# A two-layer decoder trunk: late modulation sums of layer 0 behind dt's chain, layer 1's first chunk by pieces of h, scale columns at once

## The chip, the cores and the metric

One core of a Trainium2 chip runs the kernel. The metric is device time in microseconds (us) of one launch, the median of several runs. The engines are TensorE (PE in the profile; PEld are its weight loads), VectorE (DVE), ScalarE (ACT), GpSimd (POOL), and SyncE (SP), on whose queue the loads are issued.

## The reference, cut to what matters

The input is 256 tokens of width 1024, all in float32. Two layers follow each other, and both do this:

```python
cond = silu(c)
mod = cond @ ada_w[l] + ada_b[l]              # 6 x 1024: sh1, sc1, g1, sh2, sc2, g2
h = rms_norm(x, norm1_g[l]) * (1 + sc1) + sh1
z, xbc, dt_raw, mq, mk, mv, sq, sk, sv = split(h @ w_in[l])
y_ssd  = ssd_mixer(z, conv(xbc), softplus(dt_raw + bias), ...)   # two chunks of 128 tokens
y_moba = moba_attention(mq, mk, mv)           # with 256 tokens: plain causal attention, 4 heads
y_swa  = swa_attention(sq, sk, sv)            # window 128, with sinks, 4 heads
x = x + g1 * (concat(rms_norms of the three) @ w_out[l])
h = rms_norm(x, norm2_g[l]) * (1 + sc2) + sh2
x = x + g2 * peer_ffn(h)                      # 8 heads, top 16 of 128 x 128 experts
```

A last RMSNorm follows.

## The kernel before

**Tiling.** Channels lie on partitions in eight blocks of 128 (KD = 8), tokens in two blocks (NC = 2). Products in float32 are made in two ways. The first projections of a layer multiply float32 as it is (`proj_parts_whole`, `proj_tokens_whole`, lines 360 and 375). All others split each operand into a high and a low part in fp32r: `split` (lines 165 to 177) copies the high part on ScalarE and subtracts for the low part, on VectorE in layer 1 and on GpSimd in layer 0 (`low_of`), and `mm3` multiplies three times (lines 180 to 182). `hs` holds the two parts of h, `wH` and `wL` those of a weight chunk, with three buffers each; `raw` holds loaded chunks in five.

**Modulations.** They are dot products on VectorE. `ada_ahead` (lines 194 to 213) makes a list of steps; one step issues the load of a weight tile of 512.5 KB three steps ahead and then one VectorE instruction (line 192), called a sum here, which multiplies the tile by the conditioning row and accumulates one column of `modc`. Layer 0 has 40 such steps in its mixers: 16 early ones (shift and scale of the first norm) and 24 late ones (m = 2, the gate of the mixers; m = 3 and 4, shift and scale of the second norm), eight columns each. Their tiles use four buffers (tags oH and oL, two each), which the last two splits of w_out use later. Layer 1's sums run in layer 0's expert stage, so layer 1's mixers have none.

**The first chunk.** h is made in four pieces p of two blocks: `norm_banks` transposes on PE into one bank, `norm_h` first makes a scale column (line 264) and then h from the bank, half on VectorE (line 284) and half on ScalarE (line 282). In layer 0 the early steps are spread over the four pieces, and five weight chunks (`WHOLE0`) are multiplied by each piece as it comes. In layer 1 the table `FIRST` says which step of the chunks mq, mk and sq goes ahead of a piece and which behind it; mq is multiplied as it is, mk and sq by high and low parts, whose `halves` of h are made in between (lines 290 and 291).

**The late steps.** After the first chunk `tick` is set to `later` (line 586), and each weight chunk that is then loaded calls it (lines 326, 354, 371), which runs two late steps (RATE). In layer 0 that starts in the stage `rest`, which computes dt and the values of attention (`values_dt`, line 609). `rest` has four chunks, so eight late steps are traced ahead of dt's chain (lines 612 to 631). The output projection calls `later` four times more (line 745).

**Order.** `ORDER` names the stages in the order in which they are traced: c0 to c3 the convolutions, mv and mp the values and output of the first attention, ss, sv and sp the scores, values and output of the second, seg the decays, z0 and z1 the gate, tok, stb, cb and st the SSD steps. What is traced first has precedence; a planner, which simulates the time of each instruction, puts one queue in order for each engine, and an engine runs its queue in that order. `tc.issue_after(i)` puts the instructions of its block behind i in the queue of the engine of i. Loads are all on SP's queue, where one that waits for its buffer holds up those behind it. Loads of `rest` are issued behind the last load of a sum that was asked for by then (line 369).

**Around it.** The output projection (lines 731 to 760) needs the gate row from m = 2; the second norm (lines 761 to 766) needs m = 3 and 4. Layer 1 starts with the end of layer 0's expert stage: lines 1080 to 1085 add it to x, and `norm_rows` and `norm_scaled` make the rows of the norm.

Of the kernel before, what the change touches and what calls it, by code (L numbers as in the profile page):

```python
# [13 lines left out]
F32 = mybir.dt.float32  # L14
# [3 lines left out]
ALU = mybir.AluOpType  # L18
# [4 lines left out]
P = 128  # L23
D = 1024
S = 256
NC = 2
KD = D // P
# [12 lines left out]
NCAND = 80  # L40
GH = 4
RB = 5
RATE = 2.0
PT = (0, 0)
CV = (1, 0)
WHOLE0 = "mq mk sq xbc0 xbc1"
FIRST = (
    ((WHOLE0, WHOLE0), ("", WHOLE0), (WHOLE0, WHOLE0), ("", WHOLE0)),
    (("- - - mq", "mq"), ("mk mk - sq sq", "mq mk sq"), ("mq - mk -", "mq mk"), ("sq sq", "mq mk sq")),
)  # L50
ORDER = (
    "rest c0 c1 mv ss mp seg c2 z0 sv c3 tok stb z1 cb st sp",
    "rest c0 mv c1 mp seg ss c2 z0 sv c3 tok stb z1 cb st sp",
)
low_of = ["h"]
# [21 lines left out]
COLS = {"adab": 0, "n1": 48, "n2": 56, "cw": 64, "cb": 96, "mg": 104}  # L77
# [13 lines left out]
def trunk(ctx: ExitStack, tc: tile.TileContext, x_in, c_in, ada, cols, rows, w_in, w_out, wq, keysT, uT, vT, fg, out, dbg=None):  # L91
    nc = tc.nc
    V, A, G, T = nc.vector, nc.scalar, nc.gpsimd, nc.tensor
# [3 lines left out]
    st = ctx.enter_context(tc.tile_pool(name="st", bufs=2))  # L97
# [56 lines left out]
    def fetch_whole(src):  # L154
# [7 lines left out]
        nc.sync.dma_start(t[:, :n], src)  # L162
        return t[:, :n]

    def split(src, low="v", pool=None):
        n = src.shape[-1]
        if pool is None:
            h = st.tile([P, 1024], F32R, tag="wH", name="wH", bufs=HB)
            lo = st.tile([P, 1024], F32R, tag="wL", name="wL", bufs=HB)
        else:  # L170
            h = pool.tile([P, D + 1], F32R, tag="oH", name="oH", bufs=2)
            lo = pool.tile([P, D + 1], F32R, tag="oL", name="oL", bufs=2)
        A.copy(h[:, :n], src)  # L173
        eng, step = (V if low == "v" else G), (n // 2 if low == "h" else n)
        for o in range(0, n, step):
            eng.tensor_tensor(out=lo[:, o:o + step], in0=src[:, o:o + step], in1=h[:, o:o + step].bitcast(F32), op=ALU.subtract)  # L176
        return h, lo

    def mm3(o, l, r, start, stop):
# [59 lines left out]
    whole2, whole2_halves = [], []  # L239
# [3 lines left out]
    def pinned():  # L243

        return tc.issue_after(pin[0]) if PIN else nullcontext()

    def norm_scaled(pool, xt, c, r):
        t = pool.tile([P, D], F32, tag="sc", name="xn", bufs=2)
        for n in range(2):
            V.tensor_scalar(out=t[:, n * 512:(n + 1) * 512], in0=xt[:, c, n * 512:(n + 1) * 512], scalar1=r, scalar2=None, op0=ALU.mult)  # L250
        return t

    def norm_banks(xn, k20=0, n=KD // 2, kind=None):
        banks = [bank(kind) for _ in range(n)]
        for c in range(NC):
            for k in range(2 * k20, 2 * (k20 + n)):
                o = k % 2 * S + c * P
                T.transpose(banks[k // 2 - k20][:, o:o + P], xn[c][:, k * P:(k + 1) * P], ident)
        return banks

    def norm_h(pool, banks, colt, modc, gcol, sh, sc, k20=0, whole=None, keep32=None):
        k0, n = 2 * k20, 2 * len(banks)
        acol = pool.tile([P, KD], F32, tag="acol", name="acol")
        V.scalar_tensor_tensor(out=acol[:, k0:k0 + n], in0=modc[:, sc, k0:k0 + n], scalar=1.0, in1=colt[:, gcol + k0:gcol + k0 + n], op0=ALU.add, op1=ALU.mult)
        halves = []
        for k2 in range(k20, k20 + len(banks)):
            if keep32 is not None:
                h32 = keep32.tile([P, 2, S], F32, tag="wt", name="h32", bufs=KD // 2)
            elif whole is None or k20 or len(banks) == 1:
                h32 = pool.tile([P, 2, S], F32, tag="t2k", name="h32", bufs=3)  # L270
            elif k2 % 2 == 0:
                four = st.tile([P, 1024], F32, tag="wL", name="h32", bufs=HB).rearrange("p (k t) -> p k t", k=4)
                h32 = four[:, 0:2, :]
            else:
                h32 = four[:, 2:4, :]
            if whole is not None:
                whole.append(h32)
            for q in range(2):
                k = 2 * k2 + q
                src = banks[k2 - k20][:, q * S:(q + 1) * S]  # L280
                if q and H32A:
                    A.activation(h32[:, q, :], src, AF.Identity, scale=acol[:, k:k + 1], bias=modc[:, sh, k:k + 1])
                else:
                    d = V.tensor_scalar(out=h32[:, q, :], in0=src, scalar1=acol[:, k:k + 1], scalar2=modc[:, sh, k:k + 1], op0=ALU.mult, op1=ALU.add)
                    done[0] = d.ins
                    if whole is not None and len(banks) > 1:
                        pin[0] = d.ins

            def half(k2=k2, h32=h32):
                A.copy(hs[0][:, 2 * k2:2 * k2 + 2, :], h32)  # L290
                V.tensor_tensor(out=hs[1][:, 2 * k2:2 * k2 + 2, :], in0=h32, in1=hs[0][:, 2 * k2:2 * k2 + 2, :].bitcast(F32), op=ALU.subtract)
            if whole is None:
                half()
            else:
                halves.append(half)
        return halves
# [19 lines left out]
    tick = [lambda: None]  # L316
# [74 lines left out]
    def mixers(l, xp, mx, xt, xn, modc, colt, early, late):  # L391
        if True:
# [54 lines left out]
            o = 0  # L447
# [69 lines left out]
                    put_y(self.yn, self.blk0, 2)  # L517

            todo = list(late)
            due = [0.0]  # L520

            def later():
                due[0] += RATE
                while todo and due[0] >= 1.0:
                    due[0] -= 1.0
                    todo.pop(0)()

            xbcT = new([P, 8, S], "xbcT")

# [22 lines left out]
            if l:  # L552
                first = {n: [bank(b) for b in kinds] for n, kinds in (("mq", ("pa", "pa")), ("mk", ("pa", "pa")), ("sq", ("pb", "pb")))}
                part = {n: proj_parts(pcs, wl, *off[n], 2) for n, pcs in first.items()}
                whole = []
                part["mq"] = proj_parts_whole(first["mq"], wl, *off["mq"], 2, whole)
            else:
# [4 lines left out]
                for n in WHOLE0.split():  # L562
# [2 lines left out]
                    first[n] = [pc[:, b * S:(b + 1) * S] for b in range(2)]  # L565
                    part[n] = proj_parts_whole(first[n], wl, *off[n], 2, whole, True)
            halves = []
            for p, names in enumerate(FIRST[l]):
                banks = norm_banks(xn, p, 1, "pc")
                pre, post = names  # L570
                pre = pre.split()
                ada = early[4 * p:4 * p + 4]
                for i in range(max(len(pre), len(ada))):
                    if i < len(ada):
                        ada[i]()
                    if i < len(pre) and pre[i] != "-":
                        with pinned() if p == 1 else tc.issue_after(asked[0]) if p == 2 and l == 0 else nullcontext():
                            next(part[pre[i]])
                halves += norm_h(xp, banks, colt, modc, COLS["n1"], 0, 1, p, whole, None if l else mx)
                for n in post.split():  # L580
                    next(part[n])
                    while l and halves:
                        halves.pop(0)()
            for g in part.values():
                assert next(g, None) is None
            tick[0] = later
            if l == 0:
                proj_tokens_rest = lambda: proj_tokens_whole(wl, *off["rest"], whole)
            else:
# [19 lines left out]
            def values_dt():  # L609

                for c, pc in enumerate(proj_tokens_rest()):
                    V.tensor_tensor(out=dtp[:, c, :], in0=pc[:, 0:8], in1=rowt[:, 0:8], op=ALU.add)
                    A.copy(vx[:, c, :, 0:64], pc[:, 8:392].rearrange("p (h d) -> p h d", d=64))


                na = new([P, NC, 8], "na")
                V.tensor_scalar(out=na, in0=dtp, scalar1=-1.0, scalar2=None, op0=ALU.mult)
                V.tensor_tensor(out=na, in0=na, in1=dtp, op=ALU.min)
                ey = new([P, NC, 8], "ey")
                A.activation(ey, na, AF.Exp)  # L620
                e1 = new([P, NC, 8], "e1")
                V.tensor_scalar(out=e1, in0=ey, scalar1=1.0, scalar2=None, op0=ALU.add)
                er = new([P, NC, 8], "er")
                V.tensor_scalar(out=er, in0=e1, scalar1=1.0, scalar2=None, op0=ALU.subtract)
                V.tensor_tensor(out=er, in0=ey, in1=er, op=ALU.subtract)
                A.activation(e1, e1, AF.Ln)
                V.tensor_tensor(out=er, in0=er, in1=e1, op=ALU.add)
                V.scalar_tensor_tensor(out=dt, in0=dtp, scalar=0.0, in1=er, op0=ALU.max, op1=ALU.add)
                ah = new([P, 8], "ah")
                A.activation(ah, rowt[:, 8:16], AF.Exp)  # L630
                V.scalar_tensor_tensor(out=a, in0=dt, scalar=-1.0, in1=ah[:, None, :].to_broadcast([P, NC, 8]), op0=ALU.mult, op1=ALU.mult)

            def decays():

# [55 lines left out]
            def swa_scores():  # L690
# [12 lines left out]
                "sv": lambda: att["s"].values(), "sp": lambda: att["s"].put(),  # L703
                "c0": lambda: conv(0), "c1": lambda: conv(1), "c2": lambda: conv(2), "c3": lambda: conv(3),
                "z0": lambda: gate_z(0), "z1": lambda: gate_z(1),
                "seg": decays, "tok": tokens, "stb": state_in, "cb": scores_cb, "st": state,
            }
            for name in ORDER[l].split():
                stages[name]()
# [53 lines left out]
                    gated_add(xp, xt, c, n, pcs[n][c], gb)  # L763
                xn.append(norm_scaled(xp, xt, c, norm_rows(xp, xt, c)))
            whole2[:] = []
            whole2_halves[:] = norm_h(xp, norm_banks(xn), colt, modc, COLS["n2"], 3, 4, 0, whole2)


    def peer(l, steps):
# [391 lines left out]
```

## Time and profile before

| | |
|---|---|
| median of 3 runs | 1942.69 us (1938.9 to 1942.85) |
| profiled execution | 1945.66 us, span 1943.9 us |
| PE busy | 1879.8 us, 97% of the span |
| DVE, ACT, POOL busy | 72%, 48%, 22% |
| mean granted clock of TensorE | 0.983 of full speed |

A busy share is a mean over the whole span. The forty slices of the profile's page (48.6 us each) show where PE is less busy: among the first four slices, and in two from 972 us on, where layer 1 starts. A row of the view of stretches gives from and to, the length, the busy time of PE, PEld, DVE, ACT and POOL with the number of records, the granted clock as a share of full speed, the share of the transfer engines and what they moved. In a timeline a row gives the start in us, the length in us, engine and line, what is written from what, and how many instructions in a row were merged; in square brackets stand the idle time ahead of it and what ended it. A float32 matmul has two records. Sums leave two entries in the trace, the product and the reading of the accumulator.

### The profile page before, as it was taken

The numbers are of one execution on the slowest core, as the hardware profiler recorded it, in microseconds if no ns is written. First come the engines' busy times: TensorE is split into PE (matmuls) and PEld (weight loads), VectorE is DVE, ScalarE is ACT, GpSimd is POOL, SyncE is SP. The second block draws the span as 40 slices with busy tenths as digits, with TensorE's granted clock in tenths as the row PEclk, the third lists the DMA queues.
The fourth block names the chain that finished last, engine by engine and source line by source line (L and its number), as shares of the span: only waits on it lengthen the run. The fifth ranks groups of instructions, "written<-read, shape, count | busy, mean of one in ns | idle before, by whom it ended". The sixth has DMA issues, their size and how long they took to land. (4 is left out here: it accounts for less than half of the span.)

```text
span 1943.9 us, 33211 instructions
## 1 busy us (share of the span) xinstructions
PE 1879.8 (97%) x12714; PEld 1707.9 (88%) x12714; DVE 1403.6 (72%) x2686; ACT 939.6 (48%) x1473; POOL 420.2 (22%) x255
## 2 busy tenths in 40 slices
PE   7798999999999999999989899999999999999998
PEld 5577999999999888888878789999999998888886
DVE  5955897889963898966657659968899346666665
ACT  2453545544444544545537444455444444555554
POOL 1263789100014001000001147960000320000000
PEclk8889999999999999999999999999999999999999
DMA  9833455444455999865543344554444555665563
GB/s 351 323 126 123 163 167 189 165 158 155 161 165 183 373 357 346 319 205 195 194 129 113 128 148 161 186 184 153 162 154 162 175 184 194 224 196 194 192 194 118
DMA packets 103984, 377.55 MB, mean 194 GB/s; under 512 B 12049, under 2 KB 12305, under 8 KB 103313
## 3 DMA queue, kind: packets, MB, share of 16 engines
q1 hardware_dynamic: 103824, 375.43, 57.1%
q8 instruction: 99, 1.62, 0.4%
q14 instruction: 61, 0.49, 0.1%
HBM read 372.24 MB, written 3.15 MB: 193 GB/s over the span
## 5 line engine op out<-in xcount | busy, mean ns | idle before, releaser
L173 ACT CAST wH<-raw 128x1024 fp32r<-128x1024 f32 x577 | 602.6, 1045 | 517.2 <-PE pu L181 349.1
L176 DVE TENSOR_TENSOR wL<-raw,wH 128x1024 fp32r<-128x1024 f32 (+1 forms) x435 | 532.9, 1226 | 215.7 <-ACT wH L173 214.7
L180 PE MATMUL pu<-hH,wH 128*128 128x256 f32 x2048 | 581.1, 284 | 6.0 <-ACT act L791 6.0
L182 PE MATMUL pu<-hH,wL 128*128 128x256 f32 x2048 | 575.7, 281 | 0.0
L181 PE MATMUL pu<-hL,wH 128*128 128x256 f32 x2048 | 575.3, 281 | 0.0
L176 POOL TENSOR_TENSOR wL<-raw,wH 128x1024 fp32r<-128x1024 f32 (+1 forms) x178 | 365.2, 2071 | 641.0 <-ACT wH L173 620.9
L181 PE MATMUL pacc<-wL,aH 128*128 128x512 f32 x1008 | 393.3, 390 | 0.0
L180 PEld LDWEIGHTS pu<-hH,wH 128*128 128x128 f32 x2048 | 386.4, 189 | 6.8 <-ACT act L791 6.8
L182 PE MATMUL pacc<-wH,aL 128*128 128x512 f32 x1008 | 392.4, 389 | 0.0
L181 PEld LDWEIGHTS pu<-hL,wH 128*128 128x128 f32 x2048 | 386.9, 189 | 0.0
L182 PEld LDWEIGHTS pu<-hH,wL 128*128 128x128 f32 x2048 | 386.6, 189 | 0.0
L180 PE MATMUL pacc<-wH,aH 128*128 128x512 f32 x1008 | 272.5, 389 | 0.0
L999 ACT CAST aH<-act 128x256 fp32r<-128x256 f32 x256 | 103.5, 407 | 323.5 <-PE pacc L181 323.5
L180 PEld LDWEIGHTS pacc<-wH,aH 128*128 128x128 f32 x1008 | 189.3, 188 | 39.5
L182 PEld LDWEIGHTS pacc<-wH,aL 128*128 128x128 f32 x1008 | 189.3, 188 | 39.1
L181 PEld LDWEIGHTS pacc<-wL,aH 128*128 128x128 f32 x1008 | 189.3, 188 | 38.9
L1000 DVE TENSOR_TENSOR aL<-act,aH 128x256 fp32r<-128x256 f32 x256 | 108.2, 425 | 100.1 <-ACT aH L999 99.8
L192 DVE SCALAR_TENSOR_TENSOR adaw<-adaw,crow 128x1025 f32<-128x1025 f32 x96 | 120.5, 1261 | 17.2 <-DMA adaw<-in_ada_dram 17.1
L1089 POOL TENSOR_TENSOR x<-x,fgb 128x512 f32<-128x512 f32 x2 | 2.6, 1293 | 350.0 <-ACT junk L232 350.0
L960 DVE SCALAR_TENSOR_TENSOR act<-pc,act 128x160 f32<-128x160 f32 (+30 forms) x126 | 38.5, 306 | 44.6 <-PE pc L954 44.6
L236 POOL TENSOR_TENSOR hr<-hm,mhalf 128x1 f32<-128x1 f32 x10 | 6.6, 664 | 285.8 <-DVE hm L234 285.8
L946 DVE TENSOR_TENSOR o<-iotax,idx 128x1024 f16<-128x1024 f16 x64 | 47.0, 735 | 17.2 <-ACT idx L915 17.1
(425 smaller groups left out, 2430.9 us busy)
## 6 DMA issues: line engine op xcount, KB each, us to landing
raw<-in_uT_dram SPq DMA_DIRECT2D x256, 512.0 KB, 3.6
raw<-in_vT_dram SPq DMA_DIRECT2D x256, 512.0 KB, 4.4
adaw<-in_ada_dram SPq DMA_DIRECT2D x96, 512.5 KB, 6.0
raw<-in_w_in_dram SPq DMA_DIRECT2D x33, 512.0 KB, 5.4
raw<-in_wq_dram SPq DMA_DIRECT2D x32, 512.0 KB, 3.6
raw<-in_w_out_dram SPq DMA_DIRECT2D x16, 512.0 KB, 3.6
whole<-in_w_in_dram SPq DMA_DIRECT2D x5, 512.0 KB, 10.5
raw<-in_w_in_dram SPq DMA_DIRECT2D x6, 392.0 KB, 3.1
```

The costliest lines, as they stand in the source:

```text
L173: A.copy(h[:, :n], src)
L176: eng.tensor_tensor(out=lo[:, o:o + step], in0=src[:, o:o + step], in1=h[:, o:o + step].bitcast(F32), op=ALU.subtract)
L180: T.matmul(o, l[0], r[0], start=start, stop=False)
L181: T.matmul(o, l[0], r[1], start=False, stop=False)
L182: T.matmul(o, l[1], r[0], start=False, stop=stop)
L192: V.scalar_tensor_tensor(out=src, in0=src, scalar=1.0, in1=cond, op0=ALU.mult, op1=ALU.mult, accum_out=modc[:, m, k:k + 1])
L236: pin[0] = G.tensor_tensor(out=r, in0=ms, in1=mhalf, op=ALU.pow).ins
L946: V.tensor_tensor(out=o1, in0=io, in1=view(idx1), op=ALU.is_equal)
L960: V.scalar_tensor_tensor(out=a, in0=pv[:, lo:hi, :], scalar=1.0 / WSCALE, in1=a, op0=ALU.mult, op1=ALU.mult)
L999: A.copy(aH, act)
L1000: V.tensor_tensor(out=aL, in0=act, in1=aH.bitcast(F32), op=ALU.subtract)
L1089: (V if c else G).tensor_tensor(out=xt[:, c, cs], in0=xt[:, c, cs], in1=fgb[:, cs], op=ALU.mult)
```

## The change

Three edits. (1) In layer 0 the chunks call the late steps no more. A stage `ada`, named eight times in `ORDER`, runs two late steps each time, behind `seg`; the other eight run in the output projection's four calls. All 24 sums are put behind `a`, the last instruction of dt's chain, in VectorE's queue. Their loads are not (the three that the early steps ask for ahead stay where they are). (2) In layer 1 only mq is multiplied by pieces; mk and sq follow in full behind the fourth piece, and the low halves of their weights are put behind the last instruction of h in VectorE's queue. (3) The scale column is a function of its own. Layer 1's first norm makes all eight columns at once, ahead of the pieces; the second norm's, already one instruction, is traced ahead of its transposes. (`scaled` is set and not used.)

```diff
-RATE = 2.0
 FIRST = (
     ((WHOLE0, WHOLE0), ("", WHOLE0), (WHOLE0, WHOLE0), ("", WHOLE0)),
-    (("- - - mq", "mq"), ("mk mk - sq sq", "mq mk sq"), ("mq - mk -", "mq mk"), ("sq sq", "mq mk sq")),
+    (("mq", "mq"), ("", "mq"), ("mq", "mq"), ("", "mq")),
 )
 ORDER = (
-    "rest c0 c1 mv ss mp seg c2 z0 sv c3 tok stb z1 cb st sp",
+    "rest c0 c1 mv ss mp seg ada c2 ada ada z0 ada ada sv c3 ada ada tok stb z1 ada cb st sp",
     "rest c0 mv c1 mp seg ss c2 z0 sv c3 tok stb z1 cb st sp",
 )
...
+    hold = [None]
     def split(src, low="v", pool=None):
...
-            eng.tensor_tensor(out=lo[:, o:o + step], in0=src[:, o:o + step], in1=h[:, o:o + step].bitcast(F32), op=ALU.subtract)
+            with tc.issue_after(hold[0]) if hold[0] else nullcontext():
+                eng.tensor_tensor(out=lo[:, o:o + step], in0=src[:, o:o + step], in1=h[:, o:o + step].bitcast(F32), op=ALU.subtract)
...
-    def norm_h(pool, banks, colt, modc, gcol, sh, sc, k20=0, whole=None, keep32=None):
-        k0, n = 2 * k20, 2 * len(banks)
+    def scale_column(pool, colt, modc, gcol, sc, k0=0, n=KD):
         acol = pool.tile([P, KD], F32, tag="acol", name="acol")
         V.scalar_tensor_tensor(out=acol[:, k0:k0 + n], in0=modc[:, sc, k0:k0 + n], scalar=1.0, in1=colt[:, gcol + k0:gcol + k0 + n], op0=ALU.add, op1=ALU.mult)
+        return acol
+
+    def norm_h(pool, banks, colt, modc, gcol, sh, sc, k20=0, whole=None, keep32=None, acol=None):
+        k0, n = 2 * k20, 2 * len(banks)
+        if acol is None:
+            acol = scale_column(pool, colt, modc, gcol, sc, k0, n)
...
                     d = V.tensor_scalar(out=h32[:, q, :], in0=src, scalar1=acol[:, k:k + 1], scalar2=modc[:, sh, k:k + 1], op0=ALU.mult, op1=ALU.add)
+                    last_h[0] = d.ins
...
-            due = [0.0]
-            def later():
-                due[0] += RATE
-                while todo and due[0] >= 1.0:
-                    due[0] -= 1.0
-                    todo.pop(0)()
+            step_ins = []
+            def later(n=2):
+                with tc.issue_after(step_ins[0]) if step_ins else nullcontext():
+                    for _ in range(n):
+                        if todo:
+                            todo.pop(0)()
...
+            acol1 = scale_column(xp, colt, modc, COLS["n1"], 1) if l else None
             for p, names in enumerate(FIRST[l]):
...
-                halves += norm_h(xp, banks, colt, modc, COLS["n1"], 0, 1, p, whole, None if l else mx)
+                halves += norm_h(xp, banks, colt, modc, COLS["n1"], 0, 1, p, whole, None if l else mx, acol1)
...
+            if l:
+                hold[0] = last_h[0]
+                for n in ("mk", "sq"):
+                    for _ in part[n]:
+                        pass
+                hold[0] = None
             for g in part.values():
                 assert next(g, None) is None
-            tick[0] = later
...
-                V.scalar_tensor_tensor(out=a, in0=dt, scalar=-1.0, in1=ah[:, None, :].to_broadcast([P, NC, 8]), op0=ALU.mult, op1=ALU.mult)
+                step = V.scalar_tensor_tensor(out=a, in0=dt, scalar=-1.0, in1=ah[:, None, :].to_broadcast([P, NC, 8]), op0=ALU.mult, op1=ALU.mult)
+                step_ins.append(step.ins)
...
+                "ada": later,
...
-            whole2_halves[:] = norm_h(xp, norm_banks(xn), colt, modc, COLS["n2"], 3, 4, 0, whole2)
+            acol2 = scale_column(xp, colt, modc, COLS["n2"], 4)
+            whole2_halves[:] = norm_h(xp, norm_banks(xn), colt, modc, COLS["n2"], 3, 4, 0, whole2, acol=acol2)
```

## Rows read from the trace of the kernel before

**Rows 1.** The page's first section: busy time, share of span, instructions, by engine.

```profile
PE 1879.8 (97%) x12714; PEld 1707.9 (88%) x12714; DVE 1403.6 (72%) x2686; ACT 939.6 (48%) x1473; POOL 420.2 (22%) x255
```

**Rows 2.** Stretches: length, busy time (records) by engine, granted clock, transfer share, GB/s.

```profile
47.70:62.50 14.80, 10.92 (x45) 8.82 (x43) 11.70 (x22) 3.69 (x9) 0.00 (x0) 0.88 1.00 384
62.50:85.20 22.70, 19.77 (x81) 13.06 (x81) 21.25 (x45) 16.28 (x27) 8.45 (x6) 0.92 0.90 319
85.20:107.40 22.20, 13.75 (x66) 10.02 (x65) 21.25 (x42) 7.64 (x20) 7.17 (x5) 0.70 0.63 211
107.40:142.40 35.00, 33.99 (x260) 31.76 (x260) 14.62 (x33) 18.63 (x33) 23.32 (x20) 1.00 0.34 113
142.40:170.30 27.90, 23.88 (x124) 19.75 (x123) 16.55 (x24) 10.37 (x20) 11.00 (x8) 0.94 0.31 104
...
200.00:985.00 785.00, 782.02 (x5439) 720.05 (x5438) 614.28 (x1162) 387.07 (x585) 165.15 (x85) 1.00 0.64 219
```

**Rows 3.** Stretches, instructions on tile adaw alone: VectorE busy (entries), clock, transfer share, GB/s.

```profile
47.70:62.50 14.80, 8.37 (x14) 0.88 1.00 384
62.50:85.20 22.70, 9.67 (x14) 0.92 0.90 319
85.20:107.40 22.20, 14.42 (x20) 0.70 0.63 211
107.40:170.30 62.90, 0.00 (x0) 0.97 0.33 109
```

**Rows 4.** Waits of PE, 47 to 180 us: total, times, longest.

```profile
PE pc L420 <- DVE yamm L217: 4.9, 1, 4.9
...
PE pb L636 <- DVE sc L475: 2.3, 1, 2.3
```

**Rows 5.** Timeline of VectorE around layer 0's last piece of h.

```profile
47.73 0.16 DVE L264 SCALAR_TENSOR_TENSOR acol<-modc,colt 128x2 f32<-128x2 f32 x1
47.81 1.22 DVE L192 SCALAR_TENSOR_TENSOR adaw<-adaw,crow 128x1025 f32<-128x1025 f32 x1
...
51.38 0.54 DVE L284 TENSOR_SCALAR h<-pc,acol,modc 128x256 f32<-128x256 f32 x1
```

**Rows 6.** Timeline of PE around layer 0's third and last pieces of h.

```profile
30.12 0.70 PE L360 MATMUL pa<-h,raw 128*128 128x256 f32 x2 [0.72 <-DVE h L284]
...
45.76 1.89 PE L360 MATMUL pa<-h,whole 128*128 128x256 f32 x8
...
51.97 0.70 PE L360 MATMUL pa<-h,whole 128*128 128x256 f32 x2 [3.88 <-DVE h L284]
...
54.51 2.88 PE L360 MATMUL pa<-h,whole 128*128 128x256 f32 x8
```

**Rows 7.** Timeline of VectorE, the end of layer 0's dt chain.

```profile
85.02 0.18 DVE L631 SCALAR_TENSOR_TENSOR a<-dt,ah 128x16 f32<-128x16 f32 x1
```

**Rows 8.** Timelines of VectorE and GpSimd: a sum beside GpSimd, and GpSimd alone.

```profile
101.27 2.06 DVE L192 SCALAR_TENSOR_TENSOR adaw<-adaw,crow 128x1025 f32<-128x1025 f32 x1
...
100.75 1.49 POOL L642 TENSOR_TENSOR segr<-mle,a 128x512 f32<-128x512 f32 x1 [0.93 <-PE pa L644]
...
109.68 1.04 POOL L642 TENSOR_TENSOR segr<-mle,a 128x512 f32<-128x512 f32 x1 [3.53 <-PE pa L644]
```

**Rows 9.** Waits of SP's queue, 0 to 180 us: total, times, longest.

```profile
SPq L204 <- DVE adaw L192: 34.2, 22, 5.3
```

**Rows 10.** Stretches of layer 1, columns as in rows 2.

```profile
1000.00:1016.00 16.00, 16.00 (x123) 15.22 (x121) 5.25 (x7) 6.13 (x12) 0.00 (x0) 1.00 0.37 117
...
1040.00:1060.00 20.00, 17.37 (x98) 12.74 (x97) 12.71 (x26) 14.90 (x24) 5.22 (x5) 0.91 0.26 85
```

**Rows 11.** Timeline of VectorE ahead of layer 1's first norm.

```profile
987.35 1.22 DVE L176 TENSOR_TENSOR wL<-raw,wH 128x1024 fp32r<-128x1024 f32 x1
988.48 0.69 DVE L303 TENSOR_TENSOR x<-x,xg 128x512 f32<-128x512 f32 x1
```

**Rows 12.** Timeline of PE at layer 1's first pieces.

```profile
992.30 1.11 PE L258 MATMUL pc<-ident,xn 128*128 128x128 f32 x4 [5.16 <-DVE xn L250]
```

More of the change, by code (lines that the diff above doesn't have):

```diff
@@ L245, in pinned @@
         return tc.issue_after(pin[0]) if PIN else nullcontext()
+    scaled, last_h = [None], [None]
     def norm_scaled(pool, xt, c, r):
@@ L249, in norm_scaled @@
         for n in range(2):
-            V.tensor_scalar(out=t[:, n * 512:(n + 1) * 512], in0=xt[:, c, n * 512:(n + 1) * 512], scalar1=r, scalar2=None, op0=ALU.mult)
+            scaled[0] = V.tensor_scalar(out=t[:, n * 512:(n + 1) * 512], in0=xt[:, c, n * 512:(n + 1) * 512], scalar1=r, scalar2=None, op0=ALU.mult).ins
         return t
@@ L705, in mixers @@
                 "z0": lambda: gate_z(0), "z1": lambda: gate_z(1),
-                "seg": decays, "tok": tokens, "stb": state_in, "cb": scores_cb, "st": state,
+                "ada": later, "seg": decays, "tok": tokens, "stb": state_in, "cb": scores_cb, "st": state,
             }
```

## The prediction

> **What bounds the kernel now.** I read the page's first section first: TensorE (PE) is busy for 97% of the span [rows 1], so only time in which it stands or runs at the lower clock can be given back. The page's forty slices put most of that in two places, the first 180 us (layer 0's mixers) and about 985 to 1120 us (layer 1's). Between them, in layer 0's expert stages, PE is busy for 782.02 of 785 us [rows 2], so what a mixer saves reaches the end. I then cut the first place by its own steps with the same view of stretches [rows 2] and asked it for the sums of the modulations alone [rows 3]. Here the reader is to see a shift in load. From 47.7 to 107.4 us VectorE is busy for 11.70 + 21.25 + 21.25 = 54.2 of 59.7 us, and the 24 late sums (14 + 14 + 20 entries, two to a sum) are 8.37 + 9.67 + 14.42 = 32.5 us of it. PE stands for 14.80 - 10.92 + 22.70 - 19.77 + 22.20 - 13.75 = 15.3 us there. From 107.4 to 170.3 us not one sum runs, and VectorE is idle for 62.9 - 14.62 - 16.55 = 31.7 us. The waits of PE name VectorE for the longest gaps [rows 4], though what PE waits for there is attention's normalisation and the mask of scores, small steps that stand in one queue with the sums. Until about 170 us then, the bound is VectorE's queue order, not its work as a whole.
>
> **Late sums behind dt's chain.** The 24 sums may now start only behind the last instruction of dt's chain (a, line 631), at 85.02 us in this trace [rows 7].
>
> First, layer 0's last piece of h. Its scale column is done at 47.73 us, then three late sums of 1.22 us run, and h comes at 51.38 [rows 5]; meanwhile PE stands for 3.88 us, where the piece before it cost only 0.72 [rows 6]. The sums gone, 3.88 - 0.72 = 3.2 us come back. Behind the gap eight matmul records took 2.88 us, where eight took 1.89 us ahead of it [rows 6]; the granted clock of the stretch is 0.88, part of it at the lower of its two levels [rows 2]. At least 2.88 - 1.89 = 1.0 us of that comes back too, and at most (1 - 0.88) x 10.92 = 1.3. Sum 4.2 us; what is late next is the weights, which PE there did not wait for.
>
> Second, 62.5 to 107.4 us. PE loses 2.93 + 8.45 = 11.4 us standing, and by the clock (1 - 0.92) x 19.77 + (1 - 0.70) x 13.75 = 5.7 us [rows 2], together 17.1. Seventeen sums, 24.1 us of VectorE, leave this stretch [rows 3] where 42.5 of 44.9 us are taken. Ahead of the chain's end at 85.02 us [rows 7] there are 9.67 us of them; the chain should end some 9 us sooner, 4 by h and about half of the 9.67. The floor of the gain is 0 (PE's order is fixed ahead, and the steps on GpSimd and ScalarE in the same chains stay), the ceiling 17.1. VectorE would be under half busy, but the chains of small steps through three engines still have gaps, so I take half: 8.5 us.
>
> Third, what it costs further on. 24 sums at 1.22 us are 29.3 us, and 32.5 by the measured sum, into a stretch with 31.7 us idle, and into whatever is idle behind dt's chain before that. VectorE's whole work from 62.5 to 170.3 us, 73.7 us, grows by the 8.4 us that come from ahead of it: 82 of some 96 us, if 12 are saved. It fits, but the idle time is cut up by convolution, attention and the SSD steps, and each sum that starts just ahead of such a step holds it for up to 1.22 us, or 2.06 beside GpSimd [rows 8]. Queued behind the held sums on VectorE are those steps and so the outputs that PE's last products need. The floor of this cost is 0; for the ceiling I let the eight sums of the output projection all fall on its chain, 8 x 2.06 = 16.5 us. I take four collisions of 1.22, 4.9 us, since the queue is planned and most steps there wait for PE, not for VectorE.
>
> Of the loads, 24 of 512.5 KB go with the sums, on SP's queue, and are moved past the loads of dt's and attention's weights. A load at its head waits for a buffer that a sum frees, 22 times for 34.2 us in all, 5.3 at most [rows 9]. Now the weights of "rest" pass ahead of them; in exchange those of c2, z0, c3, z1 and of w_out can stand behind a load whose buffer waits for a sum. Floor 0, ceiling 5.3 us once; I take 0, since the transfer share is only 0.34 and 0.31 behind 107.4 us [rows 2] and PE did not wait for weights. GpSimd's queue is passed by nothing. The last two splits of w_out use the sums' four buffers and so follow the last sum; that is inside the ceiling above.
>
> **Layer 1's start.** Only mq goes by pieces, mk and sq follow whole, and their low halves are held behind the last piece of h. PE's products are the same in number. In this trace such a half of 1.22 us runs at 987.35 us, ahead of the sum into x at 988.48 [rows 11], which the norm, and by it PE's 5.16 us of standing [rows 12], follows: 1.1 us come back, unless ScalarE's table load keeps the norm's square late, then 0. From 1000 to 1016 us PE is busy without a gap [rows 10]. Can it starve now? A piece of mq is eight records, 1.89 us at the high level [rows 6]; a piece of h is 0.54 us on VectorE [rows 5] and, by estimate, as much again on ScalarE, so pieces keep up. The four held halves are 4.9 us of VectorE, with 4 x 1.89 = 7.6 us of mq to cover them; without that cover PE would wait for the first, 1.22 us. Attention's scores need mq and mk alone and come earlier now, ahead of a stretch with 2.6 us of gaps and a clock of 0.91 [rows 10]; between 0 and 2.6 + 1.6 us, I take 1. Scale columns at once: three instructions of 0.16 us [rows 5] fewer in layer 1, beside busy PE, 0; the second norm's is issued sooner, 0. Layer 1 in all: 2.1 us, between -1.2 and 5.3.
>
> **Sum.** 4.2 + 8.5 - 4.9 + 2.1 = 9.9 us off the profiled execution's own 1945.66 us (span 1943.9 and 1.8 around it) gives 1935.8. That execution is 3.0 us over the median of the runs, 1942.69, so 1932.8 on their scale, and I say 1933.
>
> **Rivals.**
> - *More comes back.* VectorE half empty from 62.5 on, nearly all of the 17.1 us goes, say 14, and collisions cost 2: 4.2 + 14 - 2 + 2.1 = 18.3 us, 1924. For it: the longest gaps all hang on VectorE [rows 4]. Against: steps on GpSimd and ScalarE, and PE's fixed order, lie in the same chains. 0.17.
> - *The change doesn't thin the queue where it counts.* Three sums have their data long before a is done and are let go right behind it; if they and their followers fill the 20 us in which attention's normalisation is on the path, that stretch gives back 2 us instead of 8.5: 4.2 + 2 - 4.9 + 2.1 = 3.4, 1939. For it: a sum is ready as soon as it is allowed. Against: attention's steps come ahead of the sums in the script. 0.15.
> - *GpSimd becomes the bound.* A sum beside one of its products took 2.06 us instead of 1.22, and the product 1.49 instead of 1.04 [rows 8]. From 107.4 to 142.4 us GpSimd is busy for 23.32 of 35 us, with the halves of the weights that PE needs [rows 2]. Sixteen sums there at 1.49 - 1.04 = 0.45 us each add 7.2 us and bring it to 30.5, under 35 but late in places; if 5 us of it show beyond the forecast, the time is 1938. The Trainium skill, page "SBUF — State Buffer", section "Who interferes with whom", says that a VectorE instruction with two inputs from SBUF contends with a GpSimd one that reads SBUF, over an exclusively held port; by that rule, with 16 x 1.22 = 19.6 us added to 23.3, GpSimd would need 42.9 of 35 us, and 7.9 would show: about 1941. The trace agrees that both get longer, but by 0.45 and not by 1.22 us for the product. 0.06 for this.
> - *The end of the mixer gets the sums.* Place: 142.4 to 170.3 us, where VectorE is idle for 27.9 - 16.55 = 11.4 us, room for nine sums of 1.22. The sums go by four buffers, so at most four are on their way; if over nine are left at the output projection, each more holds its chain, its gate row and the splits in the sums' buffers. With 20 left, 11 x 2.06 = 22.7 us stand against the 14.8 gained: 7.9 us slower, 1950.6. For it: GpSimd is busy for 23.32 and 11.00 us beside that idle time [rows 2]. Against: 20.4 us idle on VectorE from 107.4 to 142.4 are room for sixteen. 0.17.
>
> **How the numbers follow.** Forecast 0.45 (1927 to 1939 for itself), more comes back 0.17, GpSimd 0.06, the queue not thinned 0.15, the end 0.17. About 0.2% (3.9 us) is what a measurement of this kernel can tell from no change, so faster means under 1938.8 and slower over 1946.6. Faster: 0.43 of the forecast, 0.17, 0.03 of GpSimd's case and 0.05 of the queue's, which lie on that edge: 0.68. Within it 0.02 + 0.03 + 0.10 = 0.15, slower 0.17. The range leaves out the case of the mixer's end and the far side of more coming back (both floors of cost at 0 and the ceiling of 17.1 would give 1919): 1921 to 1945.
>
> **What would show it.** Right: no sum between layer 0's last scale column and its h, PE's gap there under 1 us; a ends some 9 us sooner; VectorE under 60% busy from there to the first product of z0; sums spread over the stretch behind, with its PE gaps no more than 10 us; in layer 1 no split of a low half until the last piece of h. Wrong: gaps of PE at the output projection that end with a sum or a late gate row, or splits of POOL over 2 us each that PE waits for.

## The result: slower, and the profile after

The changed kernel takes 1953.82 us (median of 4 runs, 1952.98 to 1954.76) against 1941.79 us (4 runs, 1938.9 to 1942.85): a ratio of 1.0058, 95% interval [1.0036, 1.0079], 12.0 us slower. Forecast were 1933 us and 0.17 for slower; the time lies outside the range.

The first section of the page of after answers to [rows 1].

```profile
PE 1877.5 (96%) x12714; PEld 1706.2 (87%) x12714; DVE 1404.0 (72%) x2683; ACT 939.7 (48%) x1473; POOL 424.2 (22%) x255
```

No engine has more instructions than before (GpSimd's 255 take 4.0 us longer); the span of 1951.3 us is 7.4 longer, so PE stands 7.4 + 2.3 us more. Where, the stretches of [rows 2] show, cut at the same times in the kernel after (length, busy time and records of PE, PEld, DVE, ACT and POOL, clock, transfer share, GB/s).

```profile
47.70:62.50 14.80, 14.42 (x68) 11.14 (x69) 5.85 (x12) 7.12 (x13) 3.90 (x4) 1.00 0.73 266
62.50:85.20 22.70, 16.44 (x74) 11.95 (x73) 14.58 (x34) 13.27 (x25) 5.50 (x4) 0.92 0.47 151
85.20:107.40 22.20, 8.95 (x32) 5.26 (x33) 20.95 (x44) 7.26 (x19) 6.24 (x4) 0.55 0.84 298
107.40:142.40 35.00, 29.11 (x210) 27.79 (x210) 22.32 (x39) 11.70 (x20) 18.82 (x14) 0.84 0.49 171
142.40:170.30 27.90, 23.17 (x147) 19.92 (x146) 19.31 (x28) 13.11 (x23) 19.28 (x16) 0.99 0.40 135
200.00:985.00 785.00, 782.02 (x5484) 721.33 (x5483) 611.26 (x1180) 390.17 (x588) 171.84 (x88) 1.00 0.64 219
```

The first stretch is the gain: PE busy for 14.42 us instead of 10.92, all of it at the high level. From 85.2 to 107.4 us it is the reverse: 8.95 instead of 13.75, clock 0.55 instead of 0.70, VectorE full in both (20.95 and 21.25). From 107.4 to 142.4 us, where PE had stood for 1.0 us, it stands for 5.9. The sums alone, in the same view, answer to [rows 3] (VectorE busy, entries, clock, share, GB/s).

```profile
47.70:62.50 14.80, 0.00 (x0) 1.00 0.73 266
62.50:85.20 22.70, 5.50 (x8) 0.92 0.47 151
85.20:107.40 22.20, 14.49 (x24) 0.55 0.84 298
107.40:170.30 62.90, 13.96 (x16) 0.91 0.45 155
```

Before, they were 8.37, 9.67, 14.42 and 0.00 us. They left the first stretch and nearly half of the second, and not the third. Their order says more than these sums: a timeline of VectorE in the kernel after, from dt's chain to attention's normalised rows (start, length, engine, line, what from what).

```profile
78.97 0.18 DVE L648 SCALAR_TENSOR_TENSOR a<-dt,ah 128x16 f32<-128x16 f32 x1
79.06 1.22 DVE L194 SCALAR_TENSOR_TENSOR adaw<-adaw,crow 128x1025 f32<-128x1025 f32 x1
...
94.88 0.15 DVE L219 TENSOR_SCALAR yamm<-ss 128x1 f32<-128x1 f32 x1
94.94 1.22 DVE L194 SCALAR_TENSOR_TENSOR adaw<-adaw,crow 128x1025 f32<-128x1025 f32 x1
...
96.08 1.23 DVE L194 SCALAR_TENSOR_TENSOR adaw<-adaw,crow 128x1025 f32<-128x1025 f32 x1
...
97.31 1.23 DVE L194 SCALAR_TENSOR_TENSOR adaw<-adaw,crow 128x1025 f32<-128x1025 f32 x1
...
98.45 0.35 DVE L453 TENSOR_SCALAR ynam<-conv,yamr 128x256 f32<-128x256 f32 x1
...
119.29 2.31 DVE L194 SCALAR_TENSOR_TENSOR adaw<-adaw,crow 128x1025 f32<-128x1025 f32 x1
...
121.53 0.47 DVE L553 SCALAR_TENSOR_TENSOR conv<-pa,colt,conv 128x255 f32<-128x255 f32 x1
```

`a` comes 6.05 us sooner than in [rows 7], and the first sum starts 0.09 us behind it. All 24 then run as one train: 11 ahead of ynam (98.45), five up to attention's output (106.75), seven up to c2's first step on VectorE (121.53) and one behind that, done at 123.8 us. The last eight are written in the output projection, whose last splits come at 152.71 us. Between yamm and ynam stands one POOL step, done at 96.57 us (95.11, 1.46 us long); ynam then stands behind the sums from 96.08 and 97.31 us. The Trainium skill, page "TensorE: Matmul & The Clock Gate", section "Architectural detail: the array is 16× 32×32, not 1× 128×128", calls VectorE's queue strictly first in, first out; this trace agrees, since ynam's data are there 1.88 us before it runs. The waits of PE from 47 to 190 us in the kernel after (total, times, longest) put the same steps on its path, where [rows 4] had 4.9 us for yamm.

```profile
PE pc L430 <- DVE yamm L219: 6.5, 1, 6.5
PE pb L182 <- ACT sz L560: 5.9, 1, 5.9
...
PE pb L654 <- DVE sc L485: 3.9, 1, 3.9
```

The second names ScalarE, but it only passes VectorE's delay on. In ScalarE's timeline, the table for c2's silu is loaded when VectorE's convolution allows it, and z0's gate (sz), which empties the bank that PE waits for, stands behind that.

```profile
125.17 1.28 ACT L554 ACT_TABLE_LOAD   x1 [7.52 <-DVE conv L553]
126.46 0.42 ACT L554 ACTIVATE xbcT<-conv 128x256 f32<-128x256 f32 x1
...
128.03 0.36 ACT L560 ACTIVATE sz<-pa 128x256 f32<-128x256 f32 x1
```

**The way from mark to mark.** Five marks of VectorE cut layer 0's mixers: the last h, `a`, the first normalised rows of attention (ynam), attention's output (yL), c2's first convolution step, and the second norm's first h. Each cell gives the us from mark to mark and, in brackets, the late sums that started in between; the kernels below before and after are the experiments.

| kernel | last h at | to a | to rows | to yL | to c2 | to second h | second h at |
|---|---|---|---|---|---|---|---|
| before | 51.38 | 33.64 (11) | 12.84 (5) | 5.40 (3) | 10.72 (2) | 65.33 (0) | 179.31 |
| after | 47.48 | 31.49 (0) | 19.48 (11) | 8.30 (5) | 14.78 (7) | 67.93 (1) | 189.46 |
| e1_script_only | 47.82 | 31.26 (0) | 19.26 (11) | 8.37 (5) | 14.54 (7) | 67.95 (1) | 189.20 |
| e2_layer1_only | 50.98 | 34.80 (11) | 12.82 (5) | 5.39 (3) | 10.76 (2) | 65.37 (0) | 180.12 |
| e3_no_late_sums | 48.47 | 30.88 (0) | 6.04 (0) | 3.24 (0) | 8.90 (0) | 64.07 (0) | 161.60 |
| e4_behind_h | 48.06 | 33.87 (12) | 8.98 (3) | 6.68 (4) | 9.27 (5) | 66.27 (0) | 173.13 |
| e5_held_by_stage | 48.33 | 31.11 (0) | 6.89 (0) | 3.24 (0) | 10.03 (2) | 83.56 (22) | 183.16 |
| e6_short_sums | 47.53 | 32.06 (0) | 10.09 (7) | 3.88 (1) | 9.30 (6) | 68.55 (10) | 171.41 |
| e7_behind_attention | 48.81 | 31.73 (0) | 6.03 (0) | 3.25 (0) | 16.29 (9) | 72.56 (15) | 178.67 |
| e8_behind_h_rate1 | 48.12 | 34.05 (12) | 13.10 (5) | 6.54 (4) | 9.04 (3) | 65.91 (0) | 176.76 |
| e9_eight_and_sixteen | 47.90 | 34.02 (8) | 6.38 (0) | 4.56 (0) | 15.67 (8) | 66.84 (8) | 175.37 |
| e10_twelve_and_twelve | 47.79 | 37.07 (12) | 6.78 (0) | 4.55 (0) | 13.57 (7) | 65.38 (5) | 175.14 |

(In before and e2_layer1_only, three more sums run ahead of the last h.) The layer 0 of e1_script_only is that of after, the layer 0 of e2_layer1_only that of before: their cells repeat to within 1.2 us, and the second h to within 0.8. After against before, the second h comes -3.90 (last h) - 2.15 + 6.64 + 2.90 + 4.06 + 2.60 = 10.15 us later. The profiled pair ends 7.4 us apart, the medians 12.0.

### The profile page after: what moved, and what is told of

Same layout as the page of the kernel before. It is cut to its first block, busy times and chain, and to the rows that moved or that the text cites. A ratio compares the mean times of both kernels' runs of the same rounds, so it can differ in the third digit from the quotient of the medians.

```text
span 1951.3 us, 33215 instructions
## 1 busy us (share of the span) xinstructions
PE 1877.5 (96%) x12714; PEld 1706.2 (87%) x12714; DVE 1404.0 (72%) x2683; ACT 939.7 (48%) x1473; POOL 424.2 (22%) x255
```

## The experiments

All were timed against the kernel before on the same chip.

**One edit alone: the late sums.** The kernel after with layer 1's `FIRST`, its held halves and the scale columns as before:

```diff
-    (("mq", "mq"), ("", "mq"), ("mq", "mq"), ("", "mq")),
+    (("- - - mq", "mq"), ("mk mk - sq sq", "mq mk sq"), ("mq - mk -", "mq mk"), ("sq sq", "mq mk sq")),
...
-            acol1 = scale_column(xp, colt, modc, COLS["n1"], 1) if l else None
+            acol1 = None
```

> Edit 1 alone: layer 0's late sums by the script behind dt's chain, layer 1 and the scale columns as before. Theory (the planner lets the held sums go in one run right behind dt's chain, and attention's normalisation and c2's convolution stand behind them on VectorE): the whole loss is here, 10 to 14 us over before. Rival (layer 1's start loses it: there the granted clock fell to 0.82 from 1000 to 1016 us): at most 6 us over before.

Measured: 1953.6 us, ratio 1.0055 [1.0041, 1.0070]; second h at 189.20 us. The whole loss is this edit.

**The other two alone.** The late sums as before, the rest as after:

```diff
-                "ada": later,
...
+            tick[0] = later
```

> Edits 2 and 3 alone: layer 1's first chunk and the scale columns, late sums as before. Theory: within 3 us of before, 0 to 3 us faster, since the trace after has attention's first scores of layer 1 as late against the layer's first transposes as the trace before. Rival (layer 1 is the loss): 6 us or more slower.

Measured: 1942.97 us, ratio 1.0001 [0.9991, 1.0012]. Layer 1's 2.1 us are not in the time.

**No late sums.** The kernel after without the 24 sums and their loads; the columns they make are a constant:

```diff
-[(0, (0, 1), mod[0])] + [(0, (m,), mod[0]) for m in (2, 3, 4)]
+[(0, (0, 1), mod[0])]
...
+    G.memset(mod[0][:, 2:5, :], 0.5)
```

> The changed kernel without layer 0's 24 late sums and their loads; the gate of the mixers and the second norm's shift and scale of layer 0 are a constant 0.5. Theory: the sums cost what PE stands for in the first mixers, so 15 to 28 us under before. Rival (the waits behind dt's chain are those of ScalarE, GpSimd and PE's own order, and the sums only fill them): within 6 us of the changed kernel, over 1947.

Measured: 1927.76 us, ratio 0.9921 [0.9906, 0.9936]. So the sums cost 26 us after (1953.82 - 1927.76) and 14 us before, just short of the theory's 15; the rival fell. In the row of the stretches that answers to the worst one, PE stands for 1.1 us:

```profile
85.20:107.40 22.20, 21.12 (x154) 18.23 (x153) 7.98 (x21) 14.28 (x28) 13.95 (x13) 1.00 0.20 72
```

`a` comes at 79.35 us, no sooner than after: the rest of dt's chain isn't held by sums.

**All 24 behind the last h, in the old places.** The kernel before, with one line:

```diff
-                    todo.pop(0)()
+                    with tc.issue_after(done[0]) if l == 0 else nullcontext():
+                        todo.pop(0)()
```

> The kernel before with one thing more: layer 0's late sums stand behind the last instruction of h on VectorE, and are still called by the weight chunks. Theory: the three sums leave the place ahead of the last h and nothing is pressed together behind dt's chain: 3 to 5 us under before. Rival (what h gives back is lost again, because the three sums move into the scores and dt's chain, which stand in the same queue): within 1.5 us of before.

Measured: 1936.43 us, ratio 0.9967 [0.9955, 0.9979], faster than both kernels and by more than the theory's 3 to 5 us. Its row of the same stretch, and its timeline of VectorE at `a` and at attention's rows:

```profile
85.20:107.40 22.20, 15.24 (x70) 10.83 (x68) 19.67 (x42) 9.95 (x23) 8.32 (x7) 0.69 0.63 214
```

```profile
81.93 0.17 DVE L632 SCALAR_TENSOR_TENSOR a<-dt,ah 128x16 f32<-128x16 f32 x1
...
90.91 0.34 DVE L443 TENSOR_SCALAR ynam<-conv,yamr 128x256 f32<-128x256 f32 x1
```

The pin takes the three sums from h, which comes 3.3 us sooner; and in the queue that comes out, three sums instead of five stand between `a` and attention's rows, which gives another 3.9 us that the theory did not have. Twelve sums between h and `a` cost 33.87 - 30.88 = 3.0 us, 0.25 each (0.25 to 0.52 in all kernels that have sums there), where the change's eleven behind `a` cost 19.48 - 6.04 = 13.4 us, 1.22 each (0.98 to 1.41 in the others): about the whole length of a sum.

**The script enforced.** The kernel after, where the pin of the sums moves on with the stages: behind the last VectorE step of the stage ahead of each `ada` instead of `a` (the second line below stands at the ends of the attention's output, the convolution, `tok` and the mixers' norms).

```diff
-                step_ins.append(step.ins)
+                step_ins[:] = [step.ins]
...
+                step_ins[:] = [end.ins]
```

> The changed kernel, but each run of late sums stands on VectorE behind the last instruction of the stage that the script names ahead of it: two behind attention's output, eight behind c2's convolution, four behind c3's, two behind tok, four behind each of the two SSD outputs. Theory (it is the planner's pulling ahead that costs, not the script): between the kernel without late sums, 1928, and the one with them behind h, 1936. Rival (the mixer's end has no room for eight sums, as the prediction's last rival had it): over 1942.

Measured: 1950.14 us, ratio 1.0039 [1.0026, 1.0052]. Attention's part is cured (rows 6.89 us behind `a`), and the bill comes further on: 22 sums behind c2's first step cost 83.56 - 64.07 = 19.5 us, so the theory fell and the rival's time came. But the mixer's end is the smaller part of it. The second attention's output comes 38.27 us behind c2's first step (99.60), where e3_no_late_sums has 26.33 (from 97.53): 11.9 us for the twelve sums held behind c2's and c3's convolutions, the last of which stand right ahead of it. Timelines of VectorE, two lines of e5_held_by_stage and one of e3_no_late_sums:

```profile
136.72 1.22 DVE L194 SCALAR_TENSOR_TENSOR adaw<-adaw,crow 128x1025 f32<-128x1025 f32 x1
137.87 0.48 DVE L433 SCALAR_TENSOR_TENSOR yL<-pb,colt,yH 128x256 fp32r<-128x256 f32 x1
...
123.86 0.47 DVE L433 SCALAR_TENSOR_TENSOR yL<-pb,colt,yH 128x256 fp32r<-128x256 f32 x1
```

The other 7.6 us come from there on, with ten sums. The stretch of the mixer's end in e5_held_by_stage and its timeline there:

```profile
142.40:190.00 47.60, 37.39 (x156) 28.60 (x156) 38.01 (x64) 18.90 (x36) 10.44 (x9) 0.87 0.47 161
```

```profile
164.03 1.22 DVE L194 SCALAR_TENSOR_TENSOR adaw<-adaw,crow 128x1025 f32<-128x1025 f32 x1
...
165.44 1.21 DVE L178 TENSOR_TENSOR oL<-raw,oH 128x1024 fp32r<-128x1024 f32 x1
...
167.18 1.22 DVE L178 TENSOR_TENSOR oL<-raw,oH 128x1024 fp32r<-128x1024 f32 x1 [0.45 <-ACT oH L174]
...
174.74 0.69 DVE L312 TENSOR_TENSOR xg<-pb,gb 128x512 f32<-128x512 f32 x1 [4.50 <-PE pb L184]
```

The splits of w_out, at 142.49 and 145.50 us before, wait for the sums' buffers until 165.44; the projection's result (xg) comes 4.46 us later than in before (170.28), though c2's first step had come 14.38 us sooner.

**Short sums.** The kernel after with the late sums over 256 of 1025 columns, all loads whole:

```diff
+        if short[0] and m in (2, 3, 4):
+            src, cond = src[:, :256], cond[:, :256]
```

> The changed kernel with each late sum over 256 of 1025 columns, all loads as they are (the gate and the second norm's shift and scale of layer 0 are partial sums). Theory (VectorE's time is the cost): the sums are about 9 us instead of 32, and some three quarters of the 26 us between the changed kernel and the one without late sums come back: 1932 to 1938. Rival (the 24 loads are the cost, on SP's queue and in the transfers): 1948 or more.

Measured: 1937.07 us (1931.22 to 1941.58), ratio 0.9977 [0.9962, 0.9992]. A shorter run on VectorE alone takes 16.8 of the 26 us away; loads, positions and the remaining length (0.41 us and more) are the other 9.3, which this does not divide. By the marks 5.1 of them lie between `a` and c2, where VectorE waits for tiles of sums as well.

**All 24 behind attention's output.** The kernel after, with the pin moved:

```diff
+                if blk0 == 4:
+                    step_ins[:] = [end.ins]
```

> The changed kernel with all late sums behind the last instruction of the first attention's output instead of dt's chain. Theory (the larger half of the loss is attention's normalisation behind the sums): 1934 to 1942, with the rest of the loss still at c2's convolution. Rival (a run of 24 sums costs the same wherever it stands): 1950 or more.

Measured: 1941.84 us, ratio 1.0002 [0.9988, 1.0015]. 12.0 us less than after: that is the price of 16 sums between `a` and yL (19.48 + 8.30 - 6.03 - 3.25 = 18.5 us in the marks) less what the same sums cost later. VectorE is then full further on:

```profile
107.40:142.40 35.00, 25.96 (x170) 22.59 (x169) 33.15 (x56) 11.73 (x24) 26.44 (x16) 0.85 0.85 300
```

**Behind h at half the rate** (`RATE` 1.0 in e4_behind_h): fewer sums traced in `rest`, more behind it.

> The kernel with late sums behind h, one sum a weight chunk instead of two. Theory: fewer sums ahead of dt's chain and attention, more of them where VectorE has room: 1930 to 1936. Rival (the planner pulls them ahead all the same, as it did with the script): within 2 us of the one with two a chunk, 1936.

Measured: 1939.86 us, ratio 0.9986 [0.9974, 0.9999]. As many sums ran ahead of `a`, but five instead of three between `a` and the rows, which came at 95.27 instead of 90.91 us. Neither the theory nor the rival had this time: the planned order counts, not the rate.

**Shared out.** The kernel before, the first 8 (or, with `RATE` 3.0, 12) late sums behind h, the others behind attention's output:

```diff
+                    if l == 0 and len(todo) <= 24 - 4 * RATE and not gate:
+                        break
...
+                    with tc.issue_after(gate[0] if gate else done[0]) if l == 0 else nullcontext():
```

> The kernel before, its first eight late sums held behind layer 0's last h (as in the kernel with all 24 there, 1936.4 us) and the other sixteen behind the first attention's last output (as in the kernel with all 24 there, 1941.8). Theory (each sum costs what the small steps queued behind it in VectorE's order lose, attention's normalisation and c2's convolution being the two places): h at 48, a at about 81, attention's normalised rows at about 88 instead of 91, and its output at about 91 instead of 97.6; sixteen sums behind it cost c2's convolution and the SSD steps two thirds of the 14 us that 24 cost there, 9 us. Against the kernel without late sums, 1927.8: 2 + 9, so about 1937 to 1938, no better than all behind h. Rival (the cost behind attention grows faster than the count, since what is left over after the idle time there is what delays): sixteen fit and cost 3 us, 1933.

Measured: 1940.3 us, ratio 0.9993 [0.9981, 1.0005]. `a` (81.92) and the rows (88.30) came as the theory said, the output (92.86) 1.9 us later; the time is 2 us above its 1937 to 1938 and far from the rival's 1933.

> The same with twelve sums behind layer 0's last h and twelve behind the first attention's output. Theory: attention's output at about 93, the twelve behind it cost half of 14 us, 7, and those ahead 4: 1938 to 1939, on one line with 1936.4 (24 and 0) and 1941.8 (0 and 24). Rival: both parts fit into idle time and the time is below either end, 1932.

Measured: 1937.88 us, ratio 0.9975 [0.9964, 0.9986]: between the ends, as the theory has it; the rival's 1932 fell. Its 12 sums ahead of `a` cost 37.07 - 30.88 = 6.2 us, twice those of e4_behind_h: PE waits 6.1 us at one place for attention's scores (sc, on ScalarE behind VectorE's mask), 2.9 in e4_behind_h. So what a sum costs ahead of `a` hangs on which step it stands before, and neither of these two beats e4_behind_h.

## Why the prediction was wrong

**The step that failed is the second one, 62.5 to 107.4 us:** "Seventeen sums, 24.1 us of VectorE, leave this stretch ... I take half: 8.5 us". They did not leave it, and VectorE was busy for 14.58 + 20.95 = 35.5 of the 44.9 us there, not "under half busy". By [rows 3] 24.09 us of sums ran there before, by the rows of after 19.99, all of them behind `a`, where the path is. In place of the 8.5 us gained, the marks from the last h to yL show 7.4 us lost (-2.15 + 6.64 + 2.90). The instruction named in the pin is the only thing that holds a sum back; the eight places in `ORDER` only give precedence, and the planned queue has a sum, its tile long there or just landed, in every gap from there on. The rival "doesn't thin the queue where it counts" had this mechanism, and I argued it down with "attention's steps come ahead of the sums in the script". I also priced it too low: it left 2 us of gain where the marks show a loss of 6.64 + 2.90 us up to yL.

I had read [rows 2] as a full VectorE from 47.7 to 107.4 us and took full to mean harmful alike. It was not: before, 11 sums between h and `a` cost 33.64 - 30.88 = 2.8 us, and the five between `a` and the rows 12.84 - 6.04 = 6.8 us. The kernel without late sums shows why: there VectorE waits 16.1 us between the last h and `a`, all for ScalarE, and only 2.1 us from `a` to the rows. From yL to c2, where the change put seven sums, it waits 7.8 us. The longest entry of its waits from the last h to `a` in e3_no_late_sums (total, times, longest):

```profile
DVE conv L553 <- ACT conv L549: 13.3, 3, 7.6
```

The change moved these eleven sums from the cheap place to the dear one. What should have warned me stood in [rows 4]: the longest wait of PE was at yamm, behind `a`, so the stretch up to yL was the one to keep free, and the change put sixteen sums there instead of eight.

- *The first step, h, was right.* Timelines of VectorE and of PE at the last piece in the kernel after, which answer to [rows 5, 6]:

```profile
46.58 0.16 DVE L267 SCALAR_TENSOR_TENSOR acol<-modc,colt 128x2 f32<-128x2 f32 x1
47.48 0.54 DVE L293 TENSOR_SCALAR h<-pc,acol,modc 128x256 f32<-128x256 f32 x1 [0.74 <-PE pc L262]
```

```profile
48.08 0.70 PE L370 MATMUL pa<-h,whole 128*128 128x256 f32 x2 [0.64 <-DVE h L293]
...
49.91 1.89 PE L370 MATMUL pa<-h,whole 128*128 128x256 f32 x8
```

  No sum lies between, the gap is 0.64 us and eight records take 1.89: 3.90 us sooner for 4.2 forecast.
- *`a` "some 9 us sooner"* came 6.05 us sooner. Half of the 9.67 us of sums was to come back; by the marks 2.15 did, and e3_no_late_sums, with none, gains 0.6 us more (2.76).
- *The cost further on* was put at 4.9 us (floor 0, ceiling 16.5). The marks from yL on show 4.06 + 2.60 = 6.7 us, so this term was near in size, but not of the kind that I had counted: in place of four single collisions it is one run of seven sums ahead of c2's convolution. Part of it is the clock, low behind the standing. In PE's timeline of the kernel after, c2's products follow each other by 0.21 us (106.90, 107.11) and later by 0.12 (112.21, 112.33), the two levels:

```profile
106.90 0.41 PE L183 MATMUL pc<-hL,wH 128*128 128x256 f32 x1
107.11 0.41 PE L184 MATMUL pc<-hH,wL 128*128 128x256 f32 x1
...
112.21 0.28 PE L183 MATMUL pa<-hL,wH 128*128 128x256 f32 x1
112.33 0.28 PE L184 MATMUL pa<-hH,wL 128*128 128x256 f32 x1
```

- *The loads at 0*: SP's waits for the sums' buffers up to 180 us are 41.1 us in 26 instead of 34.2 in 22 [rows 9], the longest 5.2, and no wait of PE names a load of weights. So no cost of the loads shows apart from the sums. VectorE's own waits for their tiles, 3.1 us in five places from `a` to c2, are inside the price of the sums there, and e6_short_sums doesn't separate the two.
- *Layer 1* was put at 2.1 us, and none is in the time of e2_layer1_only (ratio 0.9991 to 1.0012). The sum into x did move ahead of the split that had stood before it in [rows 11], but the bound I had named held: ScalarE's table load comes between. Timelines of VectorE, ScalarE and PE in the kernel after:

```profile
994.56 0.69 DVE L313 TENSOR_TENSOR x<-x,xg 128x512 f32<-128x512 f32 x1
```

```profile
995.82 1.28 ACT L647 ACT_TABLE_LOAD   x1
997.12 0.21 ACT L647 ACTIVATE ah<-rowt 128x8 f32<-128x8 f32 x1
997.23 0.61 ACT L234 ACTIVATE junk<-x 128x512 f32<-128x512 f32 x1
```

```profile
999.40 1.11 PE L262 MATMUL pc<-ident,xn 128*128 128x128 f32 x4 [5.16 <-DVE xn L254]
```

  x is ready at 995.25 us, its square (junk) starts at 997.23, and PE's gap is the 5.16 us of [rows 12] to the digit. The 1 us for earlier scores did not come either: VectorE's first mask of them runs at 1023.43 us against 1016.30 before, 7.13 later, and the end of PE's gap is 7.10 later (999.40 against 992.30). Something came all the same, at neither place: from the end of PE's gap to layer 1's second h the kernel after takes 136.57 us and before 138.47. The six kernels with the old layer 1 take 138.2 to 138.8 us, five of the six with the new one 135.7 to 137.2, and e5_held_by_stage 138.6. Behind that h it is lost again: 815.33 us to the end in after, 813.13 in before. The rows of the first 10 us behind it in before and in after (columns as in [rows 2]) show a lower granted clock; from 40 to 80 us behind it the clock is 1.00 in before and 0.96 in after.

```profile
1130.77:1140.77 10.00, 10.00 (x56) 9.17 (x55) 6.57 (x10) 4.74 (x10) 1.87 (x2) 0.95 0.49 164
...
1135.97:1145.97 10.00, 10.00 (x48) 8.92 (x47) 6.66 (x10) 4.74 (x10) 0.87 (x1) 0.85 0.45 152
```

  So the 2.1 us fit in size up to layer 1's second norm, by luck, since neither of the two reasons for them held.
- *The mixer's end*, the rival for slower, lay near the time (1950.6) for another reason: after 123.8 us no sum runs in the changed kernel. Its mechanism is real once the script is enforced, for 7.6 of the 19.5 us that e5_held_by_stage loses behind c2's first step.
- *GpSimd as the bound* did not happen (18.82 of 35 us busy), but the size I had given the contention was too small (last section).

**What the marks leave over.** The second h's offset and the timed difference do not agree to better than 4 us: +10.15 and +12.0 here, +3.85 and +7.8 in e5_held_by_stage, -3.94 and -1.2 in e9_eight_and_sixteen, -6.18 and -5.9 in e4_behind_h. For the profiled pair the rest lies behind that mark, and the larger part of it is TensorE's granted clock. From layer 0's second h to the end of PE's gap at layer 1's start, before takes 812.99 us and after 809.94. The rows of the first 10 us behind that h, in before and in after, differ in the clock and in the matmul records done; from 40 to 80 us behind it the clock is 0.96 in before and 1.00 in after.

```profile
179.31:189.31 10.00, 10.00 (x47) 8.77 (x46) 6.66 (x10) 4.73 (x10) 0.72 (x1) 0.83 0.47 150
...
189.46:199.46 10.00, 10.00 (x57) 8.70 (x56) 6.57 (x10) 4.75 (x10) 1.98 (x2) 1.00 0.54 185
```

By estimate that is 0.17 x 10.00 + 0.04 x 37.92 = 3.2 us of PE's time, for the 3.05 measured. So the spans differ by 10.15 - 3.05 - 1.90 (layer 1 up to its second h) + 2.20 (behind it) = 7.4 us. The runs point the same way. Single executions of the kernel before spread from 1935.4 to 1948.3 us; of the 75 timed beside the experiments, the ten with a mean granted clock of 0.988 or more took 1935.4 to 1939.8 us, the seven with 0.983 or less 1943.5 to 1948.3. The profiled one had 0.983 and was 3.9 above the median here. What sets the clock from one execution to the next stays open.

## What to carry to other kernels

An ordering edge behind an instruction is a starting gun, not a schedule: work that is ready long before is all let go at that point, and whatever follows it in the same queue pays. Before moving filler work on an engine, price it by place, by the delay per filler between two marks of the path: here 0.25 us ahead of the end of dt's chain and 1.22 us behind it, on an engine that looked equally full in both. What tells the places apart is how long the engine waits there in a kernel without the filler, 16.1 and 2.1 us here. And hold filler out of the narrow place only (here by a pin behind h, 0.3% faster) rather than behind a later step of the path.

## What the hardware showed unexpectedly

A sum and GpSimd's splits slow each other almost as if they took turns. GpSimd's timeline in the kernel after:

```profile
114.76 7.98 POOL L178 TENSOR_TENSOR wL<-raw,wH 128x512 fp32r<-128x512 f32 x4 [1.22 <-ACT wH L174]
127.89 5.00 POOL L178 TENSOR_TENSOR wL<-raw,wH 128x512 fp32r<-128x512 f32 x4 [5.15 <-ACT wH L174]
```

Four splits take 5.00 us alone and 7.98 beside sums, and the sums beside them 1.90 to 2.31 us instead of 1.22. In these 7.98 us some 3.4 sums ran (from 115.23 us on); taking strict turns, 5.00 + 3.4 x 1.22 = 9.2 us would have been needed. The prediction had taken 0.45 us per sum for GpSimd from [rows 8]; here it is (7.98 - 5.00) / 3.4 = 0.9. That is nearer to the 1.22 that follow from the rule of the Trainium skill it cited, page "SBUF — State Buffer", section "Who interferes with whom".
